# Between two layers: expert outputs first in the loads, rows scaled by a diagonal matrix; expert flags eight to a load, overflow tables behind expert 20

## The chip, the cores and the metric

The kernel runs on one core of a Trainium2 chip. A core has five engines with an instruction queue of their own: TensorE (PE, with a sequencer PEq and a weight loader PEld), VectorE (DVE), ScalarE (ACT), GpSimd (POOL) and SyncE (SP), and 16 DMA engines which they share. The metric is the device time of one execution in microseconds (us), as the median of the runs.

## The reference

A small diffusion transformer of two layers on 512 latent rows and 256 context rows of width 1024. Each layer has a mixer (layer 0: retention and windowed attention; layer 1: a gated recurrence) and a mixture of 32 experts, of which each row takes two. What bears on the change is the experts, and what stands between them and the next layer:

```python
def hierarchical_moe(h, wg, bg, we, be, w1, w3, w2):
    ...
    e_top, e_idx = lax.top_k(e_logits, MOE_TOP_K)
    gate = g_p * jax.nn.softmax(e_top, axis=-1)
    ...
    def expert_block(args):
        xblk, e = args
        return (jax.nn.silu(xblk @ w1[e]) * (xblk @ w3[e])) @ w2[e]
    ...
def rms_norm(x, w):
    xf = x.astype(jnp.float32)
    y = xf * lax.rsqrt(jnp.mean(xf * xf, axis=-1, keepdims=True) + EPS)
    return (y * w.astype(jnp.float32)).astype(x.dtype)
```

A layer ends with x + m5 * (the sum of the two expert outputs of the row), m5 being a vector from the conditioning. The next layer normalises this row by `rms_norm`, scales and shifts it by two more such vectors, and multiplies it by the mixer's input weights.

## The kernel before

**Experts (`moe`).** All 32 experts of a layer are computed one after the other, on up to 96 gathered rows each: a first group of 64 rows (the suffix a) and, only where an expert has more than 64, a second group of 32 (the suffix b). The weights of an expert are 6 MB: two tiles of w1 and w3 (`load13`, 2 MB each) and two tiles of w2 (`load2`, 1 MB each), in loads of 1 MB on SP's queue, in a fixed order. w13 has a ring of 7 tiles, w2 one of 4, so `load2(e)` waits until PE has read expert e-2's w2 (`ya` and `yb` of e-2), and `load13(e+2)` of the next turn of the loop stands behind it in the queue. The first loads after the mixer wait for the fourth gather (`gathers[3]`), and every load is placed behind the one before it.

For expert e PE transposes gathered rows (`hga`, `hgb`, tile `xt`), multiplies them by w1 and w3 (`pa` for the first group, 32 matmuls; `pb` for the second), transposes the gated result (`gt`) and multiplies it by w2 (`ya`, `yb`). In the loop `pa` of expert e stands beside `ya` of expert e-1. Whether the second group is computed is decided at run time by a flag in the table `fl` (count over 64): PE's sequencer loads the flag into a register and branches (`when`); otherwise one matmul with zeros fills the output (`pb<-zero`, `yb<-zero`). POOL gathers the rows and scatters the weighted outputs `sa`, `sb` to `yd` in HBM.

**Overflow (`overflow`).** Rows beyond 96 of an expert go into overflow blocks. Some 22 small DVE instructions and then two one-hot matrices `osl` with 8 or 12 matmuls each (into `ov`; 24 in layer 0, 16 in layer 1) make the tables for them; a loop over `nov` blocks follows the experts. The loop calls it at expert 8 and loads `nov` at expert 16. A scheduler orders instructions of an engine by when it thinks their inputs are ready, save those that `keep_in_program_order` pins; it is free to move the overflow's work and the flag loads forward or back.

**Between the layers.** For six tiles t of 128 rows, `combine_load` loads the two expert outputs (`cy`, L1155 and L1156) and the row itself (`cxm`, L1157), SP also the vector m5 (`m5_1` for tiles 0 and 1, L316). `combine` adds the two outputs (L1164; DVE for tile 0, POOL for the others), multiplies by m5 (L1168) and adds the row (L1171), both on DVE. `rstd` sums squares on ACT (L323), DVE makes `vv` (L325), POOL raises it to -1/2 (`rr`, L327). ACT then scales the row by `rr` (`xn`, L1218), PE transposes it by an identity matrix (L1223, 8 per tile), DVE applies the vectors (L1227, L1228), and ACT and DVE split it into two half-precision parts (L1229, L1230) for the mixer's first matmuls (`pv`).

Of the kernel before, what the change touches and what calls it, by code (L numbers as in the profile page):

```python
# [8 lines left out]
F32 = mybir.dt.float32  # L9
# [4 lines left out]
ALU = mybir.AluOpType  # L14
# [11 lines left out]
CAP = 96  # L26
NOV = 16
NCOL = NE + NOV
BIG = 1.0e6
WS = 2.0 ** 10  # L30
HS = 2.0 ** 5
# [46 lines left out]


CONSTS = const_arrays()  # L80


class Kern:
# [735 lines left out]

    def overflow(s, R, mp, bank):  # L820

        nc, V, C = s.nc, s.nc.vector, s.C
        T, l = R["T"], R["l"]
        J = 2 * T
        n = [0]
# [54 lines left out]
        for g, nm in enumerate(("p64", "p32")):  # L880
            sl = mp.tile([128, J, 128], F32, name="osl")
            tt(sl, C[nm][:, None, :].to_broadcast([128, J, 128]), slot[:, :, None].to_broadcast([128, J, 128]), ALU.is_equal)
            tp = bank[:, 128 + 128 * g:128 + 128 * g + 3 * NOV]
            for j in range(J):
                s.mm(tp, sl[:, j], rhs[:, j].rearrange("p a b -> p (a b)"), j == 0, j == J - 1)
            R["otab"].append(s.table(R, tp, g, NOV, mp, f"o{g}"))
        R["oi"] = oi

# [1 line left out]
    def moe(s, l):  # L890
# [7 lines left out]
        with ExitStack() as es:  # L898
# [102 lines left out]

            def when(e, work, out):

                if e not in flag:
                    flag[e] = nc.values_load(s.R["fl"][0:1, e:e + 1], engines=[mybir.EngineType.PE], min_val=0, max_val=1)
                with tc.If(flag[e] > 0) as c:
                    work()
                with c.Else():
                    s.mm(out[:, :256], zero[:, :128], zero, True, True)
# [57 lines left out]
            pbt = lambda: psa.tile([128, 512], F32, tag="a", name="pb")  # L1067
            ybt = lambda: psy.tile([128, 512], F32, tag="y", name="yb")
            flag = {}
            gather(0, columns(0))  # L1070
            gather(1, columns(1))
            if l == 1:
# [11 lines left out]
            for e in range(NE + 1):  # L1084
                if e < NE:
                    if e + 2 < NE:
                        gather(e + 2, columns(e + 2))
                    if 0 < e < NE - 2:
                        w13.append(load13(e + 2))
                    if e > 1:  # L1090
                        w2t.append(load2(e))
                if e:
                    gate(g[e - 1], pb[e - 1], 256, 128)
                if e < NE:
                    pa = up_a(w13[e], xs[e][0])
                if e:
                    gT[e - 1] = gxpose(g[e - 1])
                if e + 1 < NE:
                    xs[e + 1] = [xpose(e + 1, 0), xpose(e + 1, 1)]
                if e < NE:  # L1100
                    g[e] = wk.tile([128, 384], F32, name="gg")
                    gate(g[e], pa, 0, 256)
                if e > 1:
                    tail_b(yb[e - 2], columns(e - 2))
                if e:
                    down_a(w2t[e - 1], gT[e - 1], columns(e - 1))
                if e < NE:
                    pb[e] = pbt()
                    when(e, lambda: up_b(pb[e], w13[e], xs[e][1]), pb[e])
                if e:  # L1110
                    yb[e - 1] = ybt()
                    when(e - 1, lambda: down_b(yb[e - 1], w2t[e - 1], gT[e - 1]), yb[e - 1])
                if e == 8:
                    s.overflow(s.R, mp, pso.tile([128, 512], F32, name="ov"))
                if e == 16:
                    nov = nc.values_load(s.R["oi"][0:1, NOV:NOV + 1], min_val=0, max_val=NOV)  # L1116
            tail_b(yb[NE - 1], columns(NE - 1))

# [29 lines left out]
            if l == 1:  # L1148
                s.final(fin, big(ra), big(ra), big(rb))

    def combine_load(s, l, t, wk, ntok):
        nc = s.nc
        r = [wk.tile([128, D], F32, name=n, bufs=b) for n, b in (("cxm", 3), ("cy0", 3), ("cy1", 3))]
        x = t if l == 0 else t + 2
        nc.sync.dma_start(r[1], s.yd[l][t * 128:(t + 1) * 128])  # L1155
        nc.sync.dma_start(r[2], s.yd[l][ntok + t * 128:ntok + (t + 1) * 128])  # L1156
        nc.sync.dma_start(r[0], s.xmid[l][x * 128:(x + 1) * 128])  # L1157
        return r

# [20 lines left out]
    def odd(s):  # L1180
        nc, tc, A = s.nc, s.tc, s.A
        V = nc.vector
        with ExitStack() as es:
# [15 lines left out]
            with s.pool("odstage", bufs=2) as st_:  # L1199
                vweights = lambda raws: [s.wsplit(None, [4, 512], pw, v=v_) for v_ in raws]  # L1200
                with tc.manual_schedule(engines={mybir.EngineType.SP}):
                    wv = vweights(s.vraw)
                    m5 = [s.mod_bc(0, 5, 1, st_, "m5_1", nc.sync)]
                    cl = [s.combine_load(0, 0, st_, NT)]
                    cl.append(s.combine_load(0, 1, st_, NT))
                    wv1 = vweights(s.vload(1))
                    m5 = [s.mod_bc(0, 5, 0, st_, "m5_0", nc.sync)] + m5
                    cl.append(s.combine_load(0, 2, st_, NT))
                for t in range(6):
# [5 lines left out]
                        nc.gpsimd.dma_start(s.xres[t * 128:(t + 1) * 128], xt)  # L1215
                    xn = st_.tile([128, D], F32, name="xn")
                    r = s.rstd(xt, xn)
                    nc.scalar.activation(xn, xt, AF.Copy, scale=r)  # L1218
                    for hf in range(2):
                        tp = ps.tile([128, 512], F32, tag="t", name="tp")  # L1220
                        for c in range(4):
                            k = hf * 4 + c
                            nc.tensor.transpose(tp[:, c * 128:(c + 1) * 128], xn[:, k * 128:(k + 1) * 128], s.ident)  # L1223
                        h32 = st_.tile([128, 4, 128], F32, name="h32")
                        bc = lambda part: fm[:, part, sti, 4 * hf:4 * hf + 4, None].to_broadcast([128, 4, 128])
                        hs = [x[:, 4 * hf:4 * hf + 4, t * 128:(t + 1) * 128] for x in hT]
# [243 lines left out]
```

## Time and profile before

| | us |
|---|---|
| median of 3 runs | 2066.09 |
| lowest and highest | 2061.59, 2066.36 |
| profiled execution | 2068.66 |
| its span in the trace | 2066.9 |
| PE busy | 1801.0 (87%) |
| DVE, ACT, POOL busy | 868.0, 562.9, 353.7 |

The mean granted clock of TensorE is 0.961 of full speed. By the trace, layer 0's experts run from about 508 to 1025 us, the step between the layers to 1115, the mixer of layer 1 to 1525 and its experts to 2030; the final norm ends the program. Of 567.73 MB that the DMA engines move, 384 loads of 1 MB are expert weights. Busy shares are means over stages with different limits, so a stage is read by its own rows.

### The profile page before, as it was taken

To read this page: it belongs to the slowest core of one execution; us is meant where nothing else is said; L and a number is where in the kernel's file an instruction comes from. 1 tells how busy PE (TensorE), PEld (TensorE's weight loads), DVE (VectorE), ACT (ScalarE), POOL (GpSimd) and SP (SyncE) were. 2 spreads that over 40 slices of the span, in tenths; PEclk is the share of its full clock that TensorE was granted. 3 is DMA by queue.
4 is the path that set the end of the run, shared out by engine and by line. 5 is a ranking of instruction groups with operands and counts; after the bars stand their busy time and mean duration, and the time that the engine had idled before them with its cause. 6 is when DMAs were issued, how large, how long until landed. Compare 5 with 4: busy or idle time off the path is not lost. (4 is left out here: it accounts for less than half of the span.)

```text
span 2066.9 us, 26460 instructions
## 1 busy us (share of the span) xinstructions
PE 1801.0 (87%) x10109; PEld 841.6 (41%) x10109; DVE 868.0 (42%) x1823; ACT 562.9 (27%) x929; POOL 353.7 (17%) x400
## 2 busy tenths in 40 slices
PE   5999999996998999888679999999869888898882
PEld 2565444454343333333234556665533333333320
DVE  5476455587211111111273597677861211112113
ACT  4356355521111111111143465464310000000000
POOL 2000000012332222221130000000142322222113
PEclk8999999998999999999979999999979999999996
DMA  9515555575999999999792221120589999999996
GB/s 320 206 45 205 184 161 206 194 265 223 360 409 371 412 412 410 411 410 415 307 315 58 66 62 43 43 73 30 208 324 399 371 377 411 408 411 411 411 402 236
DMA packets 168717, 567.73 MB, mean 275 GB/s; under 512 B 21701, under 2 KB 69310, under 8 KB 130658
## 3 DMA queue, kind: packets, MB, share of 16 engines
q1 hardware_dynamic: 145632, 523.88, 65.9%
q0 software_dynamic: 22640, 41.30, 5.6%
q8 instruction: 127, 2.08, 0.4%
q14 instruction: 44, 0.36, 0.0%
q10 hardware_dynamic: 274, 0.10, 0.0%
HBM read 554.59 MB, written 39.91 MB: 288 GB/s over the span
## 5 line engine op out<-in xcount | busy, mean ns | idle before, releaser
L144 PE MATMUL pa<-mw,xa 128*64 128x512 f32 x2048 | 540.6, 608 | 29.2 <-DMA mw<-in_moe_w 19.3
L144 PE MATMUL ya<-mw,gT 128*64 128x512 f32 x1024 | 285.8, 602 | 2.3 <-SPq L1125 1.8
L144 PEld LDWEIGHTS pa<-mw,xa 128*64 128x64 f32 x2048 | 159.5, 139 | 286.4 <-issue 279.8
L144 PE MATMUL px<-hTh,wsh 128*128 128x512 f16 (+1 forms) x672 | 226.8, 338 | 7.5 <-DVE t L438 2.8
L144 PE MATMUL px<-hTl,wsh 128*128 128x512 f16 (+1 forms) x672 | 226.9, 338 | 2.1 <-DVE hTl L348 2.0
L144 PE MATMUL px<-hTh,wsl 128*128 128x512 f16 (+1 forms) x672 | 226.6, 338 | 0.0
L144 PEld LDWEIGHTS <-wsh 128*128 128x128 f16 x1344 | 131.0, 98 | 118.7 <-issue 22.3
L939 POOL DMA_INDIRECT yd<-sb,ixm x64 | 66.8, 1044 | 549.6 <-DVE sb L1062 276.5
L1029 DVE TENSOR_TENSOR gg<-gg,pa 128x256 f32<-128x256 f32 x64 | 26.8, 419 | 296.3 <-ACT gg L1028 296.3
L1028 ACT ACTIVATE gg<-pa 128x256 f32<-128x256 f32 x64 | 24.6, 384 | 374.2 <-PE pa L144 374.2
L144 PEld LDWEIGHTS ya<-mw,gT 128*64 128x64 f32 x1024 | 79.2, 136 | 114.9 <-issue 99.2
L1029 DVE TENSOR_TENSOR gg<-gg,pb 128x128 f32<-128x128 f32 x64 | 18.4, 288 | 250.8 <-ACT gg L1028 250.8
L138 DVE SCALAR_TENSOR_TENSOR wsl<-w,wsh 128x2048 f16<-128x2048 f32 x34 | 77.7, 2288 | 37.6 <-ACT wsh L135 33.7
L1028 ACT ACTIVATE gg<-pb 128x128 f32<-128x128 f32 x64 | 17.7, 277 | 273.4 <-PE pb L144 273.4
L929 POOL DMA_INDIRECT hga<-h2d,ixm x64 | 66.8, 1043 | 118.8 <-PE xt L989 93.6
L144 PEld LDWEIGHTS <-wsl 128*128 128x128 f16 x672 | 66.2, 99 | 50.9 <-issue 5.5
L1034 PE MATMUL gt<-cca,gg 128*128 128x128 f32 x192 | 45.5, 305 | 44.8 <-DVE gg L1029 44.6
L1036 DVE COPY gT<-gt 128x384 f32<-128x384 f32 x64 | 35.4, 554 | 115.2 <-PE gt L1034 115.2
L144 PE MATMUL adaps<-adaw,cT 128*32 128x512 f32 x384 | 75.4, 639 | 3.5 <-DMA adaw<-in_ada_w 2.3
L1034 PEld LDWEIGHTS gt<-cca,gg 128*128 128x128 f32 x192 | 21.2, 140 | 137.6 <-DVE gg L1029 86.9
L939 POOL DMA_INDIRECT yd<-sa,ixm x64 | 64.2, 1003 | 65.3 <-ACT sa L1048 30.8
L144 PE MATMUL pv<-wsh,hTh 128*128 128x512 f16 (+1 forms) x192 | 69.5, 363 | 5.8 <-ACT hTh L1229 5.8
(391 smaller groups left out, 2762.4 us busy)
## 6 DMA issues: line engine op xcount, KB each, us to landing
mw<-in_moe_w SPq DMA_DIRECT2D x384, 1024.0 KB, 18.7
adaw<-in_ada_w SPq DMA_DIRECT2D x40, 1024.0 KB, 5.1
w<-in_od_w_in SPq DMA_DIRECT2D x32, 512.0 KB, 5.6
adaw<-in_ada_w SPq DMA_DIRECT2D x16, 512.0 KB, 6.0
w<-in_ev_w_in SPq DMA_DIRECT2D x8, 1024.0 KB, 6.9
cy<-yd SPq DMA_DIRECT2D x12, 512.0 KB, 9.1
xmid<-oxr POOLq DMA_DIRECT2D x10, 512.0 KB, 8.7
h2d<-ohp POOLq DMA_DIRECT2D x10, 512.0 KB, 6.0
```

Source lines behind the costliest of these rows:

```text
L138: i = s.nc.vector.scalar_tensor_tensor(lo, v, WS, hi, op0=ALU.mult, op1=ALU.subtract)
L144: return s.nc.tensor.matmul(ps, lhsT, rhs, start=first, stop=last)
L929: i = nc.gpsimd.indirect_dma_start(out=hg[e % NG][g], out_offset=None, in_=hv[g], in_offset=bass.IndirectOffsetOnAxis(ap=cols[g][0], axis= ...
L939: i = nc.gpsimd.indirect_dma_start(out=yv[g], out_offset=bass.IndirectOffsetOnAxis(ap=cols[g][1], axis=0), in_=yt, in_offset=None, bounds_ ...
L1028: nc.scalar.activation(g[:, c0:c0 + n], p[:, :n], AF.Silu)
L1029: nc.vector.tensor_tensor(g[:, c0:c0 + n], g[:, c0:c0 + n], p[:, n:2 * n], op=ALU.mult)
L1034: nc.tensor.transpose(t[:, c * 128:(c + 1) * 128], g[:, c * 128:(c + 1) * 128], s.ident)
L1036: nc.vector.tensor_copy(gT, t[:, :384])
```

## The change

It has five parts. Flags: instead of one load per flag, placed where the flag is first used, `load_flags` loads eight flags at experts 0, 8, 16 and 24, without checks of their range, and pins the loads of 8, 16 and 24 in program order. Overflow: `overflow` is called at expert 20 instead of 8, `nov` loaded at 27 instead of 16; its DVE instructions and the first matmul of each table are pinned. Loads: for the first tile the two expert outputs are loaded before m5. Scaling: instead of scaling the row by `rr` on ACT, DVE scales the identity by it (`dg`, 128x128) and PE multiplies the unscaled row by `dg`, which transposes and scales at once. By the first of these the order of the first gathers on POOL changes as well, from hga, hga, hgb, hgb to hga, hgb, hga, hgb of experts 0 and 1.

```diff
@@ class Pinned (new)
+    def __getattr__(s, name):
+        return lambda *a, **k: s.tc.keep_in_program_order(getattr(s.eng, name)(*a, **k))
@@ overflow
-        nc, V, C = s.nc, s.nc.vector, s.C
+        nc, C = s.nc, s.C
+        V = Pinned(s.tc, s.nc.vector)
...
-                s.mm(tp, sl[:, j], rhs[:, j].rearrange("p a b -> p (a b)"), j == 0, j == J - 1)
+                i = s.mm(tp, sl[:, j], rhs[:, j].rearrange("p a b -> p (a b)"), j == 0, j == J - 1)
+                if j == 0:
+                    s.tc.keep_in_program_order(i)
@@ moe
-                if e not in flag:
-                    flag[e] = nc.values_load(s.R["fl"][0:1, e:e + 1], engines=[mybir.EngineType.PE], min_val=0, max_val=1)
...
+            def load_flags(e):
+                ins, v = nc.values_load_multi_w_load_instructions(
+                    s.R["fl"][0:1, e:e + NF], engines=[mybir.EngineType.PE], min_val=0, max_val=1,
+                    skip_runtime_bounds_check_because="the result of a comparison")
+                if e:
+                    for i in ins:
+                        tc.keep_in_program_order(i)
+                flag.update({e + i: x for i, x in enumerate(v)})
...
+                    if e % NF == 0:
+                        load_flags(e)
...
-                if e == 8:
+                if e == 20:
                     s.overflow(s.R, mp, pso.tile([128, 512], F32, name="ov"))
-                if e == 16:
+                if e == 27:
                     nov = nc.values_load(s.R["oi"][0:1, NOV:NOV + 1], min_val=0, max_val=NOV)
@@ combine_load
         nc.sync.dma_start(r[2], s.yd[l][ntok + t * 128:ntok + (t + 1) * 128])
+        if between:
+            between()
         nc.sync.dma_start(r[0], s.xmid[l][x * 128:(x + 1) * 128])
@@ between the layers
-                    m5 = [s.mod_bc(0, 5, 1, st_, "m5_1", nc.sync)]
-                    cl = [s.combine_load(0, 0, st_, NT)]
+                    m5 = []
+
+                    cl = [s.combine_load(0, 0, st_, NT, lambda: m5.append(s.mod_bc(0, 5, 1, st_, "m5_1", nc.sync)))]
...
-                    nc.scalar.activation(xn, xt, AF.Copy, scale=r)
+
+                    dg = st_.tile([128, 128], F32, name="dg")
+                    V.tensor_scalar(dg, s.ident, r, None, op0=ALU.mult)
...
-                            nc.tensor.transpose(tp[:, c * 128:(c + 1) * 128], xn[:, k * 128:(k + 1) * 128], s.ident)
+                            s.mm(tp[:, c * 128:(c + 1) * 128], xt[:, k * 128:(k + 1) * 128], dg, True, True)
```

What this does to the order of instructions is shown at three places. First PE's queue in layer 0 near expert 8, before the change: flag loads (each with two checks, ISA), then the branch for `pb`.

```order
L989 MATMUL xt<-cca,hgb_4583 128x128
L1005 TENSOR_LOAD fl_4547
L1005 ISA x2
L1005 TENSOR_LOAD fl_4547
L1005 ISA x2
L1005 TENSOR_LOAD fl_4547
L1005 ISA x2
L1005 TENSOR_LOAD fl_4547
L1005 ISA x2
L1005 TENSOR_LOAD fl_4547
L1005 ISA x2
L1006 COMPARE_AND_BRANCH
```

And the same place in the changed kernel, whose lines are numbered 12 to 28 higher: the one load of eight flags, behind `ya` of the expert before and ahead of the branch for `pb`.

```order
L155 MATMUL ya<-mw,gT 64x512 [waits DMAHW5_49]
L155 MATMUL ya<-mw,gT 64x512 x3
L1084 TENSOR_LOAD fl_4547
L1018 COMPARE_AND_BRANCH
L155 MATMUL pb<-mw,xb 32x256 x32
L1018 UNCONDITIONAL_BRANCH
L155 LDWEIGHTS zero [waits Pool_49]
```

The loads of several experts in a row have become one, and `pb` of the flagged expert now stands behind `ya` of the one before it. Second, PE's queue in layer 1: in the kernel before, the first overflow matmuls stand with the first experts (behind a flag load, ahead of the rest of `pa`).

```order
L1005 TENSOR_LOAD fl_13243
L1005 ISA x2
L144 MATMUL ov<-o_14573,osl 128x48 [waits DVE_49]
L144 MATMUL ov<-o_14573,osl 128x48 x4
L144 MATMUL pa<-mw,xa 64x512 [waits DMAHW3_49,DMAHW2_49,Activation_49]
```

In the changed kernel they stand at expert 20, in the midst of its `pa`, where `o` is the right side of the tables and `osl` the one-hot matrix that DVE makes last.

```order
L155 MATMUL pa<-mw,xa 64x512 [waits DMAHW3_49,DMAHW2_49]
L155 MATMUL pa<-mw,xa 64x512 x7
L155 MATMUL ov<-o_15836,osl 128x48 [waits DVE_49]
L155 MATMUL ov<-o_15836,osl 128x48 x3
L1018 COMPARE_AND_BRANCH
L155 MATMUL pb<-mw,xb 32x256 x16
```

The overflow matmuls have moved from the first experts into expert 20, and split its `pa`; the other 12 of them follow behind this `pb` (4) and behind five more steps of `pa` (8). Third, DVE's queue between the layers, before the change, behind the sum of squares of tile 0:

```order
L1246 TENSOR_SCALAR lb<-lb 128x8 [waits DVE_49]
L325 TENSOR_SCALAR vv<-ss 128x1 [waits Activation_49]
L1227 TENSOR_TENSOR h_9403<-tp,modfm_2426 128x512 [waits PE_49]
L1228 TENSOR_TENSOR h_9403<-h_9403,modfm_2426 128x512 [waits DVE_49]
L1227 TENSOR_TENSOR h_9413<-tp,modfm_2426 128x512 [waits PE_49]
```

The same place on DVE after it:

```order
L336 TENSOR_SCALAR vv<-ss 128x1 [waits Activation_49]
L1246 TENSOR_SCALAR dg<-cca,rr 128x128 [waits Pool_49]
L1255 TENSOR_TENSOR h_9152<-tp,modfm_2426 128x512 [waits PE_49]
L1256 TENSOR_TENSOR h_9152<-h_9152,modfm_2426 128x512 [waits DVE_49]
L1255 TENSOR_TENSOR h_9162<-tp,modfm_2426 128x512 [waits PE_49]
```

And POOL's queue at this step after the change, where `cy_9103` is tile 1 and `cy_9123` tile 2:

```order
L338 TENSOR_TENSOR rr<-vv,mhalf 128x1 [waits DVE_49]
L1189 TENSOR_TENSOR cy_9103<-cy_9103,cy_9104 128x1024 [waits DMAHW1_49,DMAHW0_49]
L1189 TENSOR_TENSOR cy_9123<-cy_9123,cy_9124 128x1024 [waits DMAHW7_49,DMAHW6_49]
L1241 DMA xres<-cy_9123 128x1024 [waits DVE_49]
L338 TENSOR_TENSOR rr<-vv,mhalf 128x1 [waits DVE_49] x2
```

`dg` has come in between `vv` and the work on the transposed tile, and waits for POOL's `rr`; behind `rr` POOL's next instruction is the add of tile 1, as it was before.

## Rows read from the trace of the kernel before

**Rows 1.** The page, 40 slices of the span: busy tenths of the DMA engines.

```profile
DMA  9515555575999999999792221120589999999996
```

**Rows 2.** Waits of PE, 680 to 1016 us, then 1690 to 2030: total, times, longest.

```profile
PE pa L144 <- DMA mw<-in_moe_w: 10.0, 8, 1.5
...
PE pa L144 <- DMA mw<-in_moe_w: 9.3, 9, 1.9
```

**Rows 3.** The page, DMA issues: loads of expert weights, last column us to landing.

```profile
mw<-in_moe_w SPq DMA_DIRECT2D x384, 1024.0 KB, 18.7
```

**Rows 4.** Stretches of 10 us: busy PE, PEld, DVE, ACT, POOL; then PEclk, DMA share, GB/s.

```profile
540.00:550.00 10.00, 10.00 (x46) 3.14 (x46) 1.20 (x3) 0.93 (x3) 3.67 (x4) 1.00 0.85 301
...
640.00:650.00 10.00, 9.06 (x52) 3.18 (x41) 1.60 (x4) 1.35 (x3) 1.02 (x1) 1.00 0.57 213
...
1640.00:1650.00 10.00, 9.56 (x47) 3.44 (x43) 2.32 (x5) 1.26 (x3) 1.74 (x2) 1.00 0.76 280
1650.00:1660.00 10.00, 6.10 (x16) 1.91 (x16) 0.42 (x1) 0.00 (x0) 2.35 (x3) 0.66 1.00 383
1660.00:1670.00 10.00, 9.07 (x43) 3.28 (x41) 1.92 (x5) 0.66 (x2) 1.03 (x1) 1.00 0.62 237
```

**Rows 5.** Timeline of PE: start, duration, instruction, [idle before and releaser].

```profile
631.04 5.85 PE L144 MATMUL pa<-mw,xa 128*64 128x512 f32 x16 [3.91 <-issue]
...
1653.90 4.54 PE L144 MATMUL pa<-mw,xa 128*64 128x512 f32 x10 [3.94 <-issue]
...
1820.22 3.65 PE L144 MATMUL pa<-mw,xa 128*64 128x512 f32 x16
```

**Rows 6.** Line 1005: durations in ns, smallest, median, largest; first and last start.

```profile
L1005 PEldq TENSOR_LOAD <-fl x64: 293/301/496, 509.5 to 1654.0; - x64
```

**Rows 7.** Timelines of POOL and of SP at the start of layer 0's experts.

```profile
512.78 1.70 POOL L929 DMA_INDIRECT hga<-h2d,ixm  x1 [0.30 <-issue]
514.79 1.00 POOL L929 DMA_INDIRECT hgb<-h2d,ixm  x1 [0.30 <-issue]
...
518.39 0.81 SPq L953 DMA_DIRECT2D mw<-in_moe_w  x2
```

**Rows 8.** Timeline of PE at the second expert of layer 0.

```profile
529.02 1.21 PE L144 MATMUL ov<-o,osl 128*128 128x48 f32 x10
```

**Rows 9.** Timeline of DVE, overflow tables of layer 1: first, one-hot matrix, last.

```profile
1528.56 0.22 DVE L832 TENSOR_TENSOR o<-rpos,ccr 128x64 f32<-128x64 f32 x1
...
1531.25 1.22 DVE L832 TENSOR_TENSOR osl<-ccr,o 128x1024 f32<-128x1024 f32 x1
...
1541.42 0.28 DVE L832 TENSOR_TENSOR o<-o,rgate 128x128 f32<-128x128 f32 x1
```

**Rows 10.** Timeline between the layers, tile 0 up to its transposes.

```profile
1032.14 1.23 DVE L1164 TENSOR_TENSOR cy<-cy,cy 128x1024 f32<-128x1024 f32 x1 [2.46 <-DMA cy<-yd]
...
1037.89 2.33 POOL L1164 TENSOR_TENSOR cy<-cy,cy 128x1024 f32<-128x1024 f32 x1
1037.94 1.15 ACT L1218 ACTIVATE xn<-cy,rr 128x1024 f32<-128x1024 f32 x1 [0.87 <-POOL rr L327]
...
1039.14 1.97 PE L1223 MATMUL tp<-cca,xn 128*128 128x128 f32 x8 [19.35 <-DMA w<-in_od_w_in]
```

**Rows 11.** Timelines between the layers and of the first rows of the program.

```profile
1046.65 2.66 POOL L1164 TENSOR_TENSOR cy<-cy,cy 128x1024 f32<-128x1024 f32 x1 [6.43 <-DMA cy<-yd]
...
1047.02 3.37 DVE L1168 TENSOR_TENSOR cy<-cy,m 128x1024 f32<-128x1024 f32 x1
...
12.42 0.75 DVE L405 TENSOR_SCALAR xt<-xt,rr 128x1024 f32<-128x1024 f32 x1
...
12.56 1.02 POOL L327 TENSOR_TENSOR rr<-vv,mhalf 128x1 f32<-128x1 f32 x1 [2.04 <-DVE vv L325]
```

**Rows 12.** A product with a scalar on DVE; matmuls with as many columns (ns).

```profile
10.20 0.29 DVE L213 TENSOR_SCALAR cT<-silc 128x256 f32<-128x256 f32 x1
...
L144 PE MATMUL hs<-eq,ek x256: 222/272/377, 1168.9 to 1454.3; 128*128 128x128 f32 x64, 128*64 128x64 f32 x64
```

More of the change, by code (lines that the diff above doesn't have):

```diff
@@ L28 @@
 NCOL = NE + NOV
+NF = 8
 BIG = 1.0e6
@@ L80, with __init__ @@
 CONSTS = const_arrays()
+class Pinned:
+    def __init__(s, tc, eng):
+        s.tc, s.eng = tc, eng
+    def __getattr__(s, name):
+        return lambda *a, **k: s.tc.keep_in_program_order(getattr(s.eng, name)(*a, **k))
 class Kern:
@@ L1149, in moe, with combine_load @@
                 s.final(fin, big(ra), big(ra), big(rb))
-    def combine_load(s, l, t, wk, ntok):
+    def combine_load(s, l, t, wk, ntok, between=None):
         nc = s.nc
```

## The prediction

> **What bounds the kernel now.** I read the strip of 40 slices first: in the two stretches with the experts (slices 11 to 19 and 31 to 39) the DMA line stands at 9 nearly throughout, with the gaps that matter here shorter than a slice [rows 1]. The waits of TensorE (PE) say who ends last there: over the last two thirds of each expert stretch PE waited for weights 8 times for 10.0 us in layer 0 and 9 times for 9.3 us in layer 1 [rows 2]. So each expert stretch ends when its 192 weight loads have landed, and PE has some 10 us to spare on them. The loads sit in SP's queue, 18.7 us from issue to landing in the median [rows 3], of which one load of 1 MB takes some 2.5 us at 410 GB/s: PE can be late by about 16 us before the queue runs dry. SP waits for PE in its turn, since a ring buffer comes free only when PE has read it. A microsecond in which the DMA engines are idle is therefore lost at the end; a microsecond of PE alone is not.
>
> The table in 10 us stretches shows where the queue did run dry [rows 4]: the DMA share is 0.85 at 540 to 550, 0.57 at 640 to 650, 0.76 at 1640 to 1650 and 0.62 at 1660 to 1670. Neighbouring stretches lie at 1.00 to 1.03, so I count 1.00 as full: 1.5, 4.3, 2.4 and 3.8 us lost.
>
> **Flags, eight to a load.** Ahead of three of these four holes PE stands still with no releaser but "issue": 3.91 us before `pa` at 631.04 and 3.94 us before `pa` at 1653.90. The `pa` behind the stall also runs slower: 16 matmuls take 5.85 us at 631.04, against 3.65 us at 1820.22 [rows 5]; the granted clock of 1650 to 1660 is 0.66 [rows 4]. What PE's sequencer does meanwhile is loading flags, 64 of them in the program, 0.30 us each and two checks behind each [rows 6]; the order of before has five in a row there, and more behind them. After the change one load of eight flags stands at experts 8, 16 and 24, without checks, and one at expert 0, where PE waits for gathers anyway. The new load of eight has no row. Its price is between 0.3 us (one old load) and 8 x 0.3 = 2.4 us; I take 0.5, as it is one instruction. Either lies under the 16 us of queue from expert 16 on; at expert 8 the queue is shorter, and 2.4 us is still less than the stalls of 3.9 us and a slowed `pa` that it replaces. Gain: the three holes, 4.3 + 2.4 + 3.8 = **10.5 us**. `pb(e)` of the flagged experts moves behind `ya(e-1)`, which holds the w13 buffers longer; but the loads for them stand in SP's queue behind w2 loads that wait for `yb` already, so I price it at nothing; without that cover it would be the few us of half a `pa` and `ya`, once per layer at expert 8.
>
> **Start of the experts.** The overflow tables of before run among the expert tables: the second gather took 1.70 us where VectorE (DVE) builds `osl`, and SP's weights, which wait for the fourth gather, go on at 518.39 [rows 7]. The others take 1.00, so 0.7 us go, and a little more as the tables themselves come earlier: 0.9 in layer 0, 0.5 in layer 1, where less was in the way (bounds 0 and 1.5 each). Then the overflow matmuls leave experts 1 to 8: 10 of them, 1.21 us, stand before the second expert's `pa` [rows 8], and the gathers' new order (both halves of expert 0 first) lets PE begin about 1.2 us sooner. PE comes some 3 us earlier to the reads of weights that SP waits for behind the first experts, which covers the hole of 1.5 us at 540 to 550. In layer 1 the dips are about 0.6 us. Together 0.9 + 1.5 + 0.5 + 0.6 = **3.5 us**.
>
> **Overflow behind expert 20.** The same work returns there, pinned in program order. On DVE that is one block of 22 instructions; in before, layer 1's run from 1528.56 to 1541.42 with 9.8 us of busy time by my sum, 1.22 of it the one-hot matrix `osl` [rows 9]. In layer 1 the first four `ov` matmuls stand between the eighth and the ninth `pa` step and wait for that block, which begins only with the `gT` copy shortly before: PE stands still some 6 us, then come 16 matmuls of 0.12 us (the row's 1.21 us for 10) and a clock that has fallen, some 9 us in all. In layer 0 they stand at the end of an expert, and PE loses about 4 us. What is queued behind: `pb`, `pa`, `ya`, and SP's loads for later experts. 9 us is less than 16, so the DMA engines go on; but PE must make it up before the end, and its waits for weights in the rest of the stretch are just those 9 to 10 us [rows 2]. I take **1 us** of loss, bounds 0 and 9.
>
> **Between the layers.** With the expert outputs first, the first tile's sum of its two rows, which waited for `cy` until 1032.14 [rows 10], starts one load of 0.5 MB earlier: 1.2 us. The scaling on ScalarE (ACT), 1.15 us between `rr` and the transposes, goes away [rows 10]; in its place DVE builds `dg`. The same instruction on 128x256 takes 0.29 us [rows 12], so 128x128 takes no more; I take 0.25. The matmul against `dg` replaces a transpose of the same shape: fp32 matmuls of at most 128x128 have a median of 272 ns [rows 12], and tile 0's 8 transposes take 1.97 us [rows 10], 246 ns each, so I count them as equal. That makes 1.2 + 1.15 - 0.25 = 2.1 us for tile 0, and if tile 1's product with m5 then escapes the GpSimd (POOL) add beside it (3.37 instead of 1.22 us [rows 11]), another 2.15: 4.2 us.
>
> But look at what POOL does at the same moment: right after `rr`, at 1037.89, it starts a 2.33 us add of the next tile [rows 10], while `dg` becomes ready. Two pairs show it [rows 11]. At 1046.65 POOL's add starts, and DVE's product ends 1.08 us behind it, 3.37 us long. At 12.42 DVE is first, with the very kind of instruction that `dg` is (one tensor times a column), and POOL's `rr` takes 1.02 us for its usual 0.56 and ends 0.41 behind it. So the two exclude each other, and `dg` of tile 0 waits for the add: `rr` ends at 1037.9 - 1.2 = 1036.7, the add at 1039.0, PE starts at about 1039.2, against 1039.14 [rows 10]. Nothing is gained for tile 0. I take 1 us for the later tiles, whose path loses ACT's scaling: **1 us**, bounds 0 and 4.2. The Trainium skill, page "SBUF — State Buffer", section "SBUF: two separate sides", says that a DVE instruction with two SBUF inputs or in a two-port mode and a GpSimd instruction hold a shared pair of ports in turn, each for its whole length. By it `dg`, one input, would be held as above if it runs in such a mode: 1 us; if not, 4.2. No row of before has a one-input product arriving second.
>
> **Sum.** 10.5 + 3.5 + 1 - 1 = 14.0 us. The profiled execution took 2068.66 us; less 14 is 2054.7. The median of the runs is 2066.09, 2.6 lower, which gives **2052 us**.
>
> **Rivals.** (1) *dg is free of the add:* 3.2 us more, 2049 us. For it: no one-input product is seen waiting; against it: 12.42. (2) *PE doesn't make up expert 20:* the full 9 us of layer 1 stay, so 8 more than taken, 2060 us. For it: PE's spare is no larger than its lateness, and DVE's and POOL's mutual waits [rows 11] could lengthen the block; against it: the spare of layer 0 is 10.0 us for 4. (3) *Only part of the holes closes:* a flagged expert still computes `pb` and `yb` there, PE is late without the flag loads, and half of the 10.5 us stays: 2057 us. Against it: the 16-matmul `pa` alone grew by 2.2 us and stood 3.9 idle. Nor would the change do what it says if the eight-flag load cost its upper 2.4 us and stalled PE again at expert 8: 2 x 2 us more, still 2056. (4) *Slower: the queue runs dry at expert 20.* Place: `ov` waiting for DVE's block in both layers. It decides once PE is late by more than 16 us, which takes a block twice as long as counted, by sharing with POOL's scatters; then every further microsecond is lost and the spare is gone too: some 10 us a layer against the 1 taken, 19 more, 2071 us.
>
> **How the numbers follow.** Chances: my sum 0.52, (1) 0.16, (2) 0.14, (3) 0.14, (4) 0.04. The sum's own range is 2046 to 2056, from the bounds at the start and between the layers. With (1) to (3) and the runs' spread of some 5 us, 2043 to 2062 leaves out no more than 2 in 10. A difference under 0.3%, 6.2 us, is about what measurement can't tell from none; (2) lies on that line, so half of it and a part of (3) are "same": faster 0.83, same 0.12, slower 0.05.
>
> **What would show it.** Flags: 64 loads become 8, the idle time "issue" at 631 and 1653 is gone, and no stretch before 1700 falls under a DMA share of 0.9. Start: SP goes on about 0.9 us sooner after the first gather. Expert 20: an idle time of some 6 us before `ov` in layer 1 with the DMA share at 1.0 beside it, and fewer waits for weights after it. Between the layers: `dg` of tile 0 as long as POOL's add beside it (2 us or more) means that the exclusion holds; 0.25 us that it doesn't. I am wrong if the holes stay with the flag loads gone, or if a new hole opens near expert 20.

## The result, and the profile after

| | median, us | lowest to highest | runs |
|---|---|---|---|
| before | 2066.17 | 2061.59 to 2074.73 | 5 |
| changed | 2055.22 | 2054.06 to 2060.58 | 5 |

The ratio of the changed kernel to the one before is 0.994 (95% interval 0.9925 to 0.9955): 10.95 us faster by the medians, where 14 were forecast. The profiled execution of the changed kernel took 2056.7 us, with a span of 2054.9 and a mean granted clock of 0.967. The page's two strips of 40 slices (granted clock, DMA engines), the second to be laid beside [rows 1]:

```profile
PEclk9999999998999999999889999999989999999996
DMA  9515545575999999999783121120589999999996
```

The DMA line reads almost as before: the gain is in gaps shorter than a slice. So to stretches of 10 us: those of [rows 4], three in which moved work now stands (630, 840, 1850), and the lowest of the changed kernel (1610). The columns are busy PE, PEld, DVE, ACT, POOL; then granted clock, DMA share, GB/s:

```profile
540.00:550.00 10.00, 9.78 (x46) 3.44 (x43) 1.79 (x4) 0.98 (x2) 3.03 (x3) 1.00 0.99 387
630.00:640.00 10.00, 8.34 (x88) 3.91 (x88) 2.17 (x5) 1.94 (x4) 3.06 (x3) 1.00 1.01 411
640.00:650.00 10.00, 9.07 (x48) 3.00 (x48) 0.71 (x2) 0.66 (x2) 1.04 (x2) 1.00 1.03 413
840.00:850.00 10.00, 10.00 (x37) 6.34 (x39) 0.54 (x3) 0.18 (x1) 1.35 (x2) 0.53 1.02 414
1610.00:1620.00 10.00, 9.79 (x71) 3.83 (x67) 1.17 (x3) 1.26 (x3) 0.45 (x1) 1.00 0.92 373
1640.00:1650.00 10.00, 9.07 (x44) 3.11 (x42) 0.91 (x2) 0.38 (x1) 1.41 (x3) 1.00 1.01 408
1650.00:1660.00 10.00, 9.06 (x44) 3.14 (x42) 2.21 (x5) 1.15 (x3) 3.77 (x4) 1.00 1.02 404
1660.00:1670.00 10.00, 8.25 (x42) 3.06 (x40) 2.54 (x5) 0.98 (x2) 3.46 (x4) 1.00 1.02 416
1850.00:1860.00 10.00, 4.71 (x24) 3.23 (x20) 6.84 (x17) 0.28 (x1) 1.16 (x1) 0.81 1.03 414
```

The holes of 0.85, 0.57, 0.76 and 0.62 are closed (0.99, 1.03, 1.01, 1.02). The same work stands 4 to 7 us earlier in this trace, so a hole could hide in a neighbouring stretch; but of all stretches from 520 to 980 and from 1530 to 1990 us the lowest is 0.92, at 1610. At expert 20 TensorE (PE) is disturbed instead: at 840 its granted clock is 0.53, near the lower of its two levels (1.2 of 2.4 GHz), and at 1850 it is busy for 4.71 of 10 us. The DMA share beside that stays at 1.02 and 1.03, which is what the forecast of that edit rested on.

The load of eight flags, in the view of its line (count, then smallest, median and largest duration in ns, first and last start):

```profile
L1084 PEldq TENSOR_LOAD <-fl x8: 592/598/780, 512.7 to 1899.4; - x8
```

0.60 us against the 0.5 that I chose, and 8 of them where [rows 6] had 64. The timelines of POOL and SP at the start of layer 0's experts answer to [rows 7]:

```profile
507.54 1.12 POOL L943 DMA_INDIRECT hga<-h2d,ixm  x1 [3.68 <-DVE ixm L815]
508.97 1.06 POOL L943 DMA_INDIRECT hgb<-h2d,ixm  x1 [0.30 <-issue]
...
511.63 1.00 POOL L943 DMA_INDIRECT hgb<-h2d,ixm  x1 [0.30 <-issue]
...
513.94 5.47 SPq L967 DMA_DIRECT2D mw<-in_moe_w  x4
```

The second gather takes 1.06 instead of 1.70 us, and SP's weights go on 513.94 - 507.54 = 6.40 us behind the first gather. Before, that gather began at 511.35, and SP went on 7.04 behind it: 0.64 us sooner, of 0.9 forecast.

PE at expert 20, timeline (start, duration, instruction, idle time before and releaser), first layer 0, then layer 1; and PE's waits, 672 to 1008 and 1680 to 2020 us (total, times, longest):

```profile
833.91 2.88 PE L155 MATMUL ov<-o,osl 128*128 128x48 f32 x24
...
839.55 5.33 PE L155 MATMUL ov<-o,osl 128*128 128x48 f32 x24 [1.42 <-DVE osl L91]
844.81 5.89 PE L155 MATMUL pa<-mw,xa 128*64 128x512 f32 x16
...
1857.20 1.94 PE L155 MATMUL ov<-o,osl 128*128 128x48 f32 x8 [5.29 <-DVE osl L91]
...
1859.15 1.78 PE L155 MATMUL ov<-o,osl 128*128 128x48 f32 x8
1860.86 3.89 PE L155 MATMUL pa<-mw,xa 128*64 128x512 f32 x10
1864.68 1.99 PE L155 MATMUL ov<-o,osl 128*128 128x48 f32 x16
```

```profile
PE pa L155 <- DMA mw<-in_moe_w: 2.9, 3, 1.5
...
PE pa L155 <- DMA mw<-in_moe_w: 3.6, 4, 1.4
```

In layer 0 PE is late by 2.88 + 1.42 + 5.33 us, and by 2.24 more as the next `pa` takes 5.89 us instead of 3.65 [rows 5]: 11.9 us, where I had 4. In layer 1 it is 5.29 + 1.94 + 1.78 + 1.99 = 11.0 us, and some 1.6 more as 10 steps of `pa` take 3.89 us, where 10 of the 16 in 3.65 would take 2.3: 12.6 us, where I had 9. The waits for weights of these last two thirds fall from 10.0 and 9.3 us [rows 2] to 2.9 and 3.6, so 7.1 and 5.7 us of the lateness are paid from them; e1 below gives the fitter comparison.

Between the layers, timeline of tiles 0 and 2 (POOL's add of the next tile, DVE's `dg`, PE's products), then the group of all these products by shape (count, busy us, mean ns of one):

```profile
1027.56 2.33 POOL L1189 TENSOR_TENSOR cy<-cy,cy 128x1024 f32<-128x1024 f32 x1
1027.61 2.37 DVE L1246 TENSOR_SCALAR dg<-cca,rr 128x128 f32<-128x128 f32 x1 [0.68 <-POOL rr L338]
1030.03 3.78 PE L155 MATMUL tp<-dg,cy 128*128 128x128 f32 x16 [19.65 <-DMA w<-in_od_w_in]
...
1049.54 0.29 DVE L1246 TENSOR_SCALAR dg<-cca,rr 128x128 f32<-128x128 f32 x1
...
1050.06 2.37 DVE L1246 TENSOR_SCALAR dg<-cca,rr 128x128 f32<-128x128 f32 x1 [0.24 <-POOL rr L338]
```

DVE's first product on the transposed tile 0 (`h`), first in the changed kernel, then in the one before:

```profile
1032.14 0.69 DVE L1255 TENSOR_TENSOR h<-tp,modfm 128x512 f32<-128x512 f32 x1 [2.17 <-PE tp L155]
```

```profile
1040.29 0.69 DVE L1227 TENSOR_TENSOR h<-tp,modfm 128x512 f32<-128x512 f32 x1 [3.04 <-PE tp L1223]
```

The group of all products in the changed kernel:

```profile
L155 PE MATMUL tp<-dg,cy 128*128 128x128 f32 x96 | 16.4, 341 | 23.8 <-DMA w<-in_od_w_in 19.6 <-DVE dg L1246 2.9 <-DVE h L1255 1.2
```

The same group of the kernel before:

```profile
L1223 PE MATMUL tp<-cca,xn 128*128 128x128 f32 x48 | 9.1, 351 | 25.2 <-DMA w<-in_od_w_in 19.4 <-ACT xn L1218 3.8 <-DVE h L1227 2.0
```

Two things stand here. `dg` takes 2.37 us where POOL's add of 2.33 us begins 0.05 us ahead of it, and 0.29 us where none does. And the mean of one record has not risen (351 and 341 ns), but there are twice as many: a product of 128x128 fp32 is two records of PE, a transpose one. Tile 0's products take 3.78 us; its transposes took 1.97 [rows 10]. Both delay tile 0: its first `h` begins 1032.14 - 1015.65 = 16.49 us behind the first load of the stage (now an expert output, before it m5), where it was 1040.29 - 1025.05 = 15.24.

### The profile page after: what moved, and what is told of

It reads as the page before. It is cut to its first block, busy times and chain, and to the rows that moved or that the text cites. A ratio compares the mean times of both kernels' runs of the same rounds, so it can differ in the third digit from the quotient of the medians.

```text
span 2054.9 us, 26368 instructions
## 1 busy us (share of the span) xinstructions
PE 1798.3 (88%) x10157; PEld 847.1 (41%) x10157; DVE 878.7 (43%) x1829; ACT 556.0 (27%) x923; POOL 354.1 (17%) x400
## 5 line engine op out<-in xcount | busy, mean ns | idle before, releaser
L155 PE MATMUL pa<-mw,xa 128*64 128x512 f32 x2048 | 534.9, 602 | 8.2 <-DMA mw<-in_moe_w 6.5
L155 PEld LDWEIGHTS ya<-mw,gT 128*64 128x64 f32 x1024 | 79.6, 136 | 112.8 <-issue 100.3
L943 POOL DMA_INDIRECT hga<-h2d,ixm x64 | 67.4, 1054 | 123.9 <-PE xt L1003 95.4
L146 ACT ACTIVATE wsh<-w 128x2048 f16<-128x2048 f32 x34 | 64.6, 1904 | 25.0 <-DMA w<-in_ev_w_in 10.4
## 6 DMA issues: line engine op xcount, KB each, us to landing
w<-in_od_w_in SPq DMA_DIRECT2D x32, 512.0 KB
adaw<-in_ada_w SPq DMA_DIRECT2D x16, 512.0 KB
cy<-yd SPq DMA_DIRECT2D x12, 512.0 KB
xmid<-oxr POOLq DMA_DIRECT2D x10, 512.0 KB
h2d<-ohp POOLq DMA_DIRECT2D x10, 512.0 KB
```

The source lines that it names most:

```text
L146: i = s.nc.scalar.activation(hi, v, AF.Copy, scale=WS)
L155: return s.nc.tensor.matmul(ps, lhsT, rhs, start=first, stop=last)
L943: i = nc.gpsimd.indirect_dma_start(out=hg[e % NG][g], out_offset=None, in_=hv[g], in_offset=bass.IndirectOffsetOnAxis(ap=cols[g][0], axis= ...
```

## The experiments

The theory: each expert stretch ends with its weight loads, so closing the stretches with a low DMA share gives the gain, PE's lateness at expert 20 is free as long as loads are queued, and between the layers the wait of `dg` for POOL's add eats what the new order of loads gives. The rivals: PE is late without the flag loads as well; the lateness at expert 20 is paid at the end; the part between the layers gains or loses on its own. Each group of runs was made on one chip, with the kernel before beside it.

| label | kernel | median (runs) | before (runs) | ratio, 95% interval |
|---|---|---|---|---|
| e1_flags_only | before, flags eight to a load | 2059.11 (8) | 2068.41 (26) | 0.9952, 0.9938 to 0.9967 |
| e2_flags_undone | changed, flags one by one | 2063.41 (10) | 2068.41 (26) | 0.9975, 0.9956 to 0.9994 |
| e3_overflow_at_8 | changed, overflow as before | 2059.83 (10) | 2068.41 (26) | 0.9961, 0.9945 to 0.9976 |
| e4_scale_on_act | changed, scaling as before | 2056.67 (7) | 2068.41 (26) | 0.9944, 0.9924 to 0.9964 |
| e5_dg_on_act | changed, `dg` made on ACT | 2051.55 (4) | 2069.45 (16) | 0.9907, 0.9884 to 0.993 |
| e6_overflow_at_12 | changed, overflow at expert 12 | 2062.63 (9) | 2069.45 (16) | 0.9965, 0.9949 to 0.9981 |
| e7_scale_on_act_again | as e4 | 2056.24 (6) | 2069.45 (16) | 0.993, 0.9914 to 0.9947 |
| e8_changed_again | changed | 2056.84 (6) | 2069.45 (16) | 0.9935, 0.9918 to 0.9952 |
| e9_between_only | before, the part between the layers | 2070.54 (12) | 2068.33 (23) | 1.0011, 0.9997 to 1.0025 |
| e10_between_dg_act | as e9, `dg` made on ACT | 2067.67 (12) | 2068.33 (23) | 1.0003, 0.9988 to 1.0018 |
| e11_dg_act_again | as e5 | 2052.76 (6) | 2068.33 (23) | 0.9929, 0.9908 to 0.9951 |

**Flags alone.** The edit on the kernel before:

```diff
-                if e not in flag:
-                    flag[e] = nc.values_load(s.R["fl"][0:1, e:e + 1], ...)
...
+            def load_flags(e):
...
+                    if e % NF == 0:
+                        load_flags(e)
```

> The kernel before with one part of the change: flags loaded eight at a time. Theory A (the time is set by the stream of weight loads, and each microsecond in which it runs dry early is lost at the end): the holes near expert 8 of both layers close, 4.5 us in layer 0 and 6 to 7 in layer 1, so some 11 us faster than before, about 2055 us; the share of the DMA engines stays at 0.95 or more from 600 to 700 us and from 1600 to 1700, and the idle time of TensorE marked issue is gone. Theory B (most of the gain comes from the overflow matmuls leaving the first experts): no more than 3 us faster, 2063 us, and holes of similar size remain.

The median is 9.3 us lower. Three stretches of 10 us, the first and the last of them holes of before, 0.57 and 0.62 in [rows 4]:

```profile
640.00:650.00 10.00, 9.32 (x93) 4.20 (x93) 1.27 (x3) 1.72 (x4) 3.31 (x4) 1.00 1.02 408
...
1620.00:1630.00 10.00, 9.26 (x72) 4.10 (x70) 3.21 (x7) 1.58 (x3) 2.06 (x2) 1.00 0.81 301
...
1660.00:1670.00 10.00, 8.91 (x41) 2.92 (x39) 0.94 (x3) 0.66 (x2) 1.02 (x1) 1.00 1.03 410
```

The holes of before are full, at 640 with `pb` and `yb` of the flagged expert still computed there (93 records of PE). So the flag loads made these holes, and rival (3) of the prediction, that half of them stays, falls. One expectation missed: at 1620 to 1630 the share is 0.81, not 0.95. That dip of 1.9 us, where `yb` of a flagged expert of layer 1 is computed, is deeper than in the kernel before, and in the changed kernel it is the 0.92 at 1610. Its cause was not followed up. PE's waits for weights in the last two thirds (678 to 1014 and 1682 to 2020 us) are as long as before, with no overflow work beside them:

```profile
PE pa L145 <- DMA mw<-in_moe_w: 10.9, 8, 3.0
...
PE pa L145 <- DMA mw<-in_moe_w: 12.4, 10, 2.7
```

Against these, the changed kernel's 2.9 and 3.6 are 8.0 and 8.8 us less, for 11.9 and 12.6 us of lateness; where the rest was made up was not followed.

**Flags undone.** In the changed kernel the single load stands in `when` again, and `load_flags` is gone.

```diff
+                if e not in flag:
+                    flag[e] = nc.values_load(s.R["fl"][0:1, e:e + 1], ...)
...
-                    if e % NF == 0:
-                        load_flags(e)
```

> The changed kernel with its flags loaded one at a time again, as before. Theory A: the holes near expert 8 come back and cost 10 to 12 us, about 2066 us, with the DMA share under 0.8 in two or three stretches of 10 us near expert 8. Theory B: 2058 us or less, since the overflow work is no longer beside the flag loads.

The holes are back, and the clock falls with them (0.66), in stretches of 10 us:

```profile
620.00:630.00 10.00, 4.76 (x14) 1.76 (x16) 0.56 (x2) 0.60 (x1) 3.07 (x3) 0.66 1.02 405
...
640.00:650.00 10.00, 8.86 (x43) 3.20 (x43) 2.18 (x5) 1.95 (x4) 4.11 (x4) 1.00 0.74 268
...
1640.00:1650.00 10.00, 7.85 (x41) 3.06 (x38) 2.46 (x5) 0.98 (x2) 4.12 (x4) 1.00 0.63 219
```

They are smaller than before: 2.6 and 3.7 us, with 4.3 and 6.2 there. The kernel loses 6.6 us to the median of e8, and some 8 to the first measurement of the changed kernel, less than the 10 to 12 expected. Put in alone and taken out alone, the flags are worth 7 to 9 us.

**Overflow at expert 8 again**, without the pins:

```diff
-                if e == 20:
+                if e == 8:
...
-                if e == 27:
+                if e == 16:
```

> The changed kernel with the overflow tables called at expert 8 and not pinned, as before. Theory A: the start of the experts loses what it won (about 2.5 us in layer 0 and 1 us in layer 1), the ends of both layers win back 2 and 1.3 us, because TensorE is no longer late by 10 to 13 us from expert 20 on; together within 2 us of the changed kernel, 2055 us. Rival C (lateness from expert 20 on is what ate the gain): 2050 us. Rival D (the overflow work in the first experts is the larger cost): 2060 us.

3.0 us slower than e8 by the medians and some 5 by the ratios, whose intervals just overlap. I had expected 2055 us; it came out as rival D had it, 2060. So moving the work away from the first experts is worth about the 2.5 us (3.5 less 1) of the forecast, if not more, and the 12 us of PE at expert 20 cost less than it brings. What they cost by themselves was not measured.

**Overflow at expert 12.** The same work at a place where, by my theory, fewer loads are queued:

```diff
-                if e == 20:
+                if e == 12:
```

> The changed kernel with the overflow tables called at expert 12 instead of 20. Theory A (what counts is whether the queue of weight loads is deep enough at the place): at expert 12 SP still waits for TensorE, so the 11 to 13 us by which TensorE comes late there open a hole in the weight stream of both layers, of 3 to 8 us each, and the time is 4 to 10 us longer than the changed kernel's, about 2062 us. Rival (TensorE only needs time to make the lateness up before the end): no hole, TensorE waits for weights some 10 us again in the last third, and the time is the changed kernel's or 2 us less.

5.8 us slower than e8. The 10 us stretches around the call:

```profile
730.00:740.00 10.00, 9.07 (x89) 3.85 (x89) 0.71 (x2) 0.66 (x2) 0.00 (x0) 1.00 0.81 333
740.00:750.00 10.00, 9.79 (x70) 3.76 (x71) 1.75 (x4) 1.56 (x3) 4.09 (x4) 1.00 0.75 274
...
1750.00:1760.00 10.00, 8.86 (x46) 3.72 (x47) 3.18 (x8) 1.16 (x3) 3.06 (x3) 1.00 0.96 370
```

Here the DMA engines stand idle for 1.9 + 2.5 us in layer 0, and for 0.4 us in layer 1, where I had expected 3 us or more. Nothing differs from the changed kernel but the expert, so the place decides. That the queue is deeper at expert 20 is the reading of it; the depth itself was not measured. This is the mechanism of rival (4), at a place where it happens.

**Scaling on ACT as before**, with the new order of loads kept; run twice.

```diff
-                    dg = st_.tile([128, 128], F32, name="dg")
-                    V.tensor_scalar(dg, s.ident, r, None, op0=ALU.mult)
+                    nc.scalar.activation(xn, xt, AF.Copy, scale=r)
...
-                            s.mm(tp[...], xt[...], dg, True, True)
+                            nc.tensor.transpose(tp[...], xn[...], s.ident)
```

> The changed kernel with ScalarE scaling the row and TensorE transposing it, as before; the expert outputs still come first in the loads. Theory A: the diagonal matrix of tile 0 took 2.37 us because GpSimd's add ran beside it, and the product with it takes 16 matmuls for 8 transposes; without both, tile 0's first vector product starts about 2 us earlier relative to its load, and the later tiles save TensorE 7 us in all, of which the part from tile 3 on counts; 2 to 4 us faster than the changed kernel, about 2052 us. Rival: the step between the layers is bound by loads and VectorE, so nothing changes beyond 1 us, 2055 us.

> The changed kernel with ScalarE scaling the row and TensorE transposing it, once more beside the changed kernel on the same chip. Theory A: 1 to 3 us faster than the changed kernel, from the step between the layers. Rival: the same.

2056.67 and 2056.24 us, beside 2056.84 of the unedited changed kernel (e8, below): the diagonal matrix on DVE neither gains nor loses anything measurable, as the rivals had it and not my theory (2 to 4 us, then 1 to 3). In the timeline of e4 the transposes of tile 0 begin 13.29 us behind the first load of the stage:

```profile
1020.85 0.34 SPq L1178 DMA_DIRECT2D cy<-yd  x1
...
1034.14 1.97 PE L1249 MATMUL tp<-cca,xn 128*128 128x128 f32 x8 [18.56 <-ACT xn L1244]
...
1035.29 0.69 DVE L1253 TENSOR_TENSOR h<-tp,modfm 128x512 f32<-128x512 f32 x1 [3.04 <-PE tp L1249]
```

In the kernel before, whose first load (m5) begins at 1025.05, it is 1039.14 - 1025.05 = 14.09 us, in the changed one 1030.03 - 1015.65 = 14.38. The order of loads gives 0.8 us of the 1.2 forecast, and `dg` on DVE takes back more than that. The first `h` begins 14.44 us behind the first load, where the changed kernel had 16.49: 1.1 of these 2.05 us lie ahead of PE's first record, in the path with the held `dg`, and 1.0 behind it, in the slower products.

**The changed kernel again**, unedited, as the neighbour of e5 to e7.

> The changed kernel again, unedited, for the spread between executions: by either theory 2055 us, 0.994 of the kernel before. In the trace the part ahead of the experts, which the change does not touch, tells how far two executions of the same instructions differ there (3.7 us in the first profile).

It repeats the first measurement, 0.9935 after 0.994, and `dg` of tile 0 is held once more:

```profile
1029.63 2.37 DVE L1246 TENSOR_SCALAR dg<-cca,rr 128x128 f32<-128x128 f32 x1 [0.68 <-POOL rr L338]
```

**dg on ACT.** One line of the changed kernel, run twice:

```diff
-                    V.tensor_scalar(dg, s.ident, r, None, op0=ALU.mult)
+                    nc.scalar.activation(dg, s.ident, AF.Copy, scale=r)
```

> The changed kernel with the diagonal matrix made on ScalarE instead of VectorE. Theory A (VectorE and GpSimd exclude each other while both read and write the on-chip memory): on ScalarE the matrix of tile 0 takes about 0.3 us although GpSimd's add runs beside it, and tile 0's transposes start about 2 us earlier after the first load of expert outputs than in the changed kernel (14.4 us there); the product still takes 16 matmuls for 8. Rival (the matrix was late for another reason, its input): it lasts 2 us or ends as late on ScalarE too. The whole time differs from the changed kernel by no more than 2 us either way.

> The changed kernel with dg on ACT, once more, since the first had four runs to compare. Theory A: 2049 to 2054 us, ratio to before 0.990 to 0.992, stage about 98 us. Rival: the four runs were lucky, 2055 to 2058 us, as the changed kernel.

2051.55 and 2052.76 us, the lowest medians of all. Timeline of e5 at tile 0:

```profile
1028.83 2.34 POOL L1189 TENSOR_TENSOR cy<-cy,cy 128x1024 f32<-128x1024 f32 x1
1028.88 0.40 ACT L1246 ACTIVATE dg<-cca,rr 128x128 f32<-128x128 f32 x1 [0.87 <-POOL rr L338]
1029.33 3.79 PE L155 MATMUL tp<-dg,cy 128*128 128x128 f32 x16 [17.24 <-DMA cxm<-xmid]
...
1031.45 0.69 DVE L1255 TENSOR_TENSOR h<-tp,modfm 128x512 f32<-128x512 f32 x1 [3.25 <-PE tp L155]
```

ACT makes `dg` in 0.40 us beside the very add that held DVE, and PE starts 1029.33 - 1017.36 = 11.97 us behind the first load, 2.4 sooner than in the changed kernel. I had expected the whole time to stay within 2 us of the changed kernel's; it is 5.3 and 4.1 us under e8 by the medians. Of the two runs the first lies lower by its ratio than the second did (0.9907, 0.9929), and the intervals of both overlap with that of e8; the six runs of e11 and the four of e5 lie between 2046.87 and 2056.28, the six of e8 between 2054.18 and 2059.6. It has the lowest medians: 2.5 to 5.3 us under the two of the changed kernel, and 17.9 and 15.6 under the kernel before beside it. That it is faster than the changed kernel rests on the medians and on the stage below; the ratios don't tell the two apart.

**The part between the layers alone**, on the kernel before, with the new order of loads, and `dg` on DVE (shown) and then on ACT:

```diff
...
-                    nc.scalar.activation(xn, xt, AF.Copy, scale=r)
+                    dg = st_.tile([128, 128], F32, name="dg")
+                    V.tensor_scalar(dg, s.ident, r, None, op0=ALU.mult)
...
-                            nc.tensor.transpose(tp[...], xn[...], s.ident)
+                            s.mm(tp[...], xt[...], dg, True, True)
```

> Kernel before with the part between the layers alone (load order, and dg on DVE). Theory A: the shorter path of tile 0 is eaten by dg's wait for POOL's add (2.37 us instead of 0.29, twice) and by the 16 matmuls per tile, so the stage from the first of its loads to the first px matmul stays within 100.3 to 102.9 us, as in the traces of the whole change, against 102.5 before, and the time within 3 us of the kernel before. Rival: these are scattered by other things and the part is worth its 4 us of path: stage under 99 us, time 4 us less. Second rival: the 7.3 us of added matmuls are paid in the stage: 105 us or more, time 3 us more.

> As the run of the between part alone, but dg made on ACT. Theory A: dg of tiles 0 and 2 no longer waits for POOL's add (0.4 us instead of 2.4), and the stage is 2 to 4.4 us shorter than with dg on DVE, some 98 us, the time 3 to 5 us under the kernel before. Rival: the gain seen in the first run with dg on ACT was scatter of the mixer's stage: stage and time within 1.5 us of the run with dg on DVE.

Alone, the part gives 2.2 us of loss by the medians (the interval of the ratio reaches from 0.6 us of gain to 5.2 of loss) with DVE, and 0.7 us of gain with ACT; neither can be told from none. In the timeline of e9 the wait is there as well, and the stage, from its first load to the first `px` (PE's matmul behind all the `pv` of the six tiles), takes 104.9 us:

```profile
1020.90 0.34 SPq L1155 DMA_DIRECT2D cy<-yd  x1
...
1033.45 2.37 DVE L1221 TENSOR_SCALAR dg<-cca,rr 128x128 f32<-128x128 f32 x1 [0.68 <-POOL rr L327]
...
1125.81 0.38 PE L144 MATMUL px<-hTh,wsh 128*128 128x512 f16 x1
```

That is outside the 100.3 to 102.9 us that my theory gave, and close to the second rival (the added matmuls are paid in the stage). With ACT it takes 99.1 us, as my theory had it, but the expected 3 to 5 us under the kernel before did not show in the median. The stage in all traces, and beside it the time from its first load to the first gather of layer 1, so with the mixer behind it:

| scaling | to the first `px`, us | to the first gather of layer 1, us |
|---|---|---|
| ACT and transposes, m5 first (before, e1) | 102.5, 102.2 | 505.7, 504.0 |
| ACT and transposes, outputs first (e4, e7) | 101.1, 100.7 | 503.2, 505.7 |
| `dg` on DVE (changed, e8, e6, e2, e3, e9) | 102.7, 102.7, 102.9, 100.8, 100.3, 104.9 | 508.1, 508.2, 508.4, 505.5, 505.2, 509.4 |
| `dg` on ACT (e5, e11, e10) | 98.3, 98.4, 99.1 | 502.8, 503.0, 500.8 |

One execution scatters by some 2 us to either side, with the same code. Even so the two ways to make `dg` don't overlap in either column, and their means lie 3.8 and 5.3 us apart. Against the means of the kernel before and e1, `dg` on DVE gives nothing to the first `px`, and 2.6 us of loss up to the gather. The doubled matmuls are the same on DVE and on ACT, and with `dg` on ACT the stage is shorter than with transposes (98.3 to 99.1 us, against 101.1 and 100.7). So it is the held `dg`, and not the matmuls, that keeps the gain away, and the second rival of e9 falls.

## Why the prediction was right, and where it was not

The two expert stretches in the same way: layer 0 from its first gather to the first load behind it, layer 1 from its first gather to the start of the last step of `ya`.

| kernels | layer 0, us | layer 1, us |
|---|---|---|
| as before there (before, e9, e10) | 513.7, 512.0, 514.4 | 496.7, 498.3, 498.4 |
| flags alone (e1) | 510.8 | 492.0 |
| all but the flags (e2) | 513.2 | 494.3 |
| overflow at 8 (e3), at 12 (e6) | 509.9, 510.9 | 491.8, 491.7 |
| all (changed, e8, e4, e7, e5, e11) | 508.1 to 509.1, mean 508.6 | 489.2 to 491.6, mean 490.4 |

- **Flags, 10.5 us forecast.** The mechanism is shown: single flag loads make the holes, eight to a load closes them. The size is 7 to 9 us by the medians; the interval of e1 (6.8 to 12.8 us) has room for 10.5. The new dip of e1 in layer 1 would make 10.5 - 1.9 = 8.6. From the means of the table they give 513.4 - 510.8 = 2.6 us in layer 0 put in alone, and 513.2 - 508.6 = 4.6 taken out alone, where the share of the hole gave 4.3; in layer 1 5.8 and 3.9, where it gave 6.2. These are single traces with some 2 us of scatter, so whether more of a closed hole is lost again behind it stays open. One reading of mine was wrong: the stall at 1653.90 lies behind the hole at 1640, and ahead of that hole PE stood still for 1.88 us, before the `pa` at 1635.21.
- **Start, 3.5 us, and overflow, 1 us of loss.** e3 shows their difference as 3.0 us by the medians, 2.7 by the table, for 2.5 forecast. SP goes on 0.64 us sooner instead of 0.9, and the hole at 540 is closed. Of the overflow, the sizes were wrong: 11.9 and 12.6 us of lateness for 4 and 9. I had read [rows 8] as 10 matmuls in 1.21 us, but a record is half of such a matmul: the 24 of layer 0 are 48 records, the 16 of layer 1 are 32. The small loss held even so: the DMA share beside it stayed at 1.02 and 1.03, as 12 to 13 us are still under the 16 us of queue that I had estimated, and PE's waits shrank, 10.0 and 9.3 us [rows 2] becoming 2.9 and 3.6. With a count that was too low by 8 and 4 us, that was luck in part: 4 us more would have used up the estimated queue. Rivals (2) and (4) fall at expert 20; e6 shows (4) at expert 12 of layer 0.
- **Expert stretches together:** 4.8 + 7.4 = 12.2 us by the means, for the 10.5 + 3.5 - 1 = 13.0 of the sum.
- **Between the layers, 1 us.** This is the step that failed. That `dg` waits for POOL's add was right (2.37 us twice in the changed kernel, and again in e8 and e9; 0.29 alone), and rival (1) falls. The Trainium skill ("SBUF — State Buffer", section "SBUF: two separate sides") states such a hold for a DVE instruction in a mode with two ports. The trace agrees with it in the length of the hold, though no row shows in which mode `dg` ran. That the later tiles gain 1 us was wrong, since two costs stood in it at too little. Tile 2's `dg` is held too, not only tile 0's. And "I count them as equal" was wrong for the matmul against `dg`: 96 records and 16.4 us for 48 and 9.1. In tile 0, where I had no change, the two make the first `h` 1.2 us later than before (16.49 and 15.24). In place of the 1 us the runs show no gain up to the first `px`, and 2.2 us of loss by the median of e9, not to be told from none. The wait is what the stage shows: with it gone and the matmuls kept it is 3.8 us shorter by the means, and the median of e10 is 2.9 us under that of e9, though the intervals overlap. The doubled matmuls are not seen in the stage, only in tile 0's own path. Why the stretch up to the gather loses more than the one up to `px` stays open.
- **The sum.** 12.2 us of gain in the experts and a loss of up to 2.6 between the layers make 9.6 to 12.2; the medians gave 10.95 and, in e8, 12.6. The forecast was 14.0. The predicted time of 2052 us is 3 lower than measured. The sum's own range of 2046 to 2056 us is wider than its bounds give: those at the start and between the layers make 2047 to 2054.5, and 2055.22 lies just outside that.

## What to carry to other kernels

Where loads in a queue set the end, look at the DMA share in short stretches, price a hole by it, and ask of any stall how many microseconds of loads are queued at that place: the overflow's work cost 6 us more at expert 12 than at expert 20. Before an operation is moved to another engine, look at what the engines beside it do in the same microsecond: a 0.3 us product on DVE became 2.4 beside an add on POOL, and the same product on ACT took 0.4. Count an fp32 matmul by its records in the trace, not by the call in the code.

## What the runs showed of the hardware

- A product of 128x128 fp32 on DVE with a column as scalar takes 2.37 us beside a POOL add of 2.33 us that began 0.05 us sooner, and 0.29 us alone. ACT's 0.40 us are the same beside it.
- An fp32 matmul of 128x128 by 128x128 is two records of PE, a transpose by the identity one. At a granted clock of about half (0.53 in 1029 to 1034 us of the changed kernel, 0.50 in 1039 to 1041 of the one before) eight of them take 3.78 and 1.97 us; at full clock, 1.00 in 1052 to 1054 us of e8, the eight matmuls take 2.02 in all:

```profile
1029.00:1034.00 5.00, 3.78 (x16) 3.49 (x16) 2.51 (x4) 0.40 (x1) 0.89 (x1) 0.53 1.07 393
```

```profile
1052.00:1054.00 2.00, 2.00 (x16) 1.81 (x16) 1.93 (x1) 0.02 (x1) 2.00 (x2) 1.00 0.38 152
```

- A load of eight flags into registers of PE takes 0.60 us, one flag 0.30 [rows 6].
- Code that is the same in two kernels ends at other times: the first gather of layer 0 starts at 511.35 us before, at 507.54 in the changed kernel, at 511.91 in e4. So 3.8 of the 12.0 us between the two spans come from ahead of the experts, and a part's worth is better read from a start inside the trace, or from medians.
